# Query and key projections as pairs by seven products, and filler products queued behind attention and scan steps

## The chip, the cores and the metric

The kernel runs on one core of a Trainium2 chip. The metric is the device time of one execution in microseconds. A core has TensorE (PE in the profile), VectorE (DVE), ScalarE (ACT), GpSimd (POOL) and SyncE (SP); here SyncE issues every transfer, all on one queue. SBUF and PSUM are the on-chip memories, PSUM with eight banks that matmuls write.

## The reference

One inference step of one layer over 1024 new and 64 running rows (T = 1088), width 1024:

```
xn = rmsnorm(x);  z, xBC, dt, q, k, v, g_ssm, g_att = split(xn @ w_in)
xBC = silu(causal_conv4(xBC) + bias);  dt = softplus(dt + bias)
y = ssd_scan(x, dt, B, C, chunks of 64) ; y = rmsnorm((y + D*x) * silu(z)) per group
q, k = partial_rope(rmsnorm per head of 64);  16 heads of q and k, 8 of v
o = rmsnorm((softmax(q1 k1) - lam * softmax(q2 k2)) v)       chunk-causal
x += (sigmoid(g_ssm) * (y @ w_bs) + sigmoid(g_att) * (o @ w_ba)) @ w_out
x += (silu(causal_conv3(a)) * b) @ w_down,  a, b = split(rmsnorm(x) @ w_up)
outputs: x, k, v, the last scan states and the last rows of both convolutions
```

Everything is fp32. The kernel writes an fp32 operand as hi + lo (hi rounded to a shorter type) and forms hi·hi, hi·lo and lo·hi, so a product of two blocks is three matmuls.

## The kernel before

Features lie on the 128 partitions and time on the free axis. `xn` (hi and lo) stays in SBUF. A projection of 128 features is a *block*. `project` computes a plain block in three parts (384, 384 and 320 columns), 24 matmuls each.

The stages in order:

1. Norm of x, then `values(0)` and `values(1)`, which also give dt. `steps` turns dt into step sizes, decays and cumulative sums (`dtt`, `nacum`, `decs`).
2. `heads` for q, then for k: eight plain blocks each. The evacuation copies every part from PSUM into a row `qr` (ten buffers of T columns in the pool `qk`), squares it and sums the squares over the blocks. After the eighth block the whole tensor is normed at once: a matmul with `blk`, `rstd_of`, a product per row, the rotation on rows 0 and 1, the split into hi and lo, and the stores to `q_st` or `k_st` in DRAM. Between the two the cached keys are split likewise. k's rows use the same ten buffers.
3. `differences` forms sums and differences of quarters of `xn` for a seven-product scheme (Winograd's form of Strassen's). `values(2)` and `values(3)` run beside it.
4. Twenty *pairs*: two blocks together (`seven`), of z or of x, B and C. Per pair there are seven products `p` on two column halves `s`, 168 matmuls of 272 columns. The weights' seven left factors (`left_blocks`) are made one pair ahead by GpSimd, ScalarE and VectorE. `Gated` applies silu to z and stores it in `z_sc`; `Conv` convolves and stores in `x_sc`.
5. Attention: eight heads, nine steps each in `ATT_ORDER`. A step is scores (matmuls into `sc`), maximum, exponentials, difference, transposes (`pt`), weighted sum (`po`). `fill(rate)` hands out parts of the *filler* beside the steps: the 16 gate blocks, 48 parts.
6. Scan: 36 steps, with a `front` (transposes `tr`, `cb`) and a `back` (`yi`, `ye`, `stp`) each. The filler goes on with the remaining gates, then with the branch products of o and of the first half of y.
7. The last branch, the output projection and the feed-forward part.

The Tile framework orders each engine's instructions by a simulated timeline, in which program order is the priority: work whose inputs are ready can move ahead of work that waits. That decides where filler matmuls stand between the steps of attention and the scan. Engines then work through their queues in that order.

Of the kernel before, what the change touches and what calls it, by code (L numbers as in the profile page):

```python
# [17 lines left out]
P = 128  # L18
# [23 lines left out]
WMAX = 4 * (256 + 16)  # L42
# [15 lines left out]
ATT_STEPS = 0.53  # L58
SCAN_STEPS = 1.08
MID = dict(fa=8, fs=2, fu=4, pr=6, cc=4)  # L60
MIDW = 552


def group(g):
# [4 lines left out]
PAIRS = [p for i in range(4) for p in (("c", CONV[6 * i], CONV[6 * i + 1]), ("z", 4 * i, 4 * i + 1),  # L69
                                       ("c", CONV[6 * i + 2], CONV[6 * i + 3]),  # L70
                                       ("c", CONV[6 * i + 4], CONV[6 * i + 5]), ("z", 4 * i + 2, 4 * i + 3))]
# [8 lines left out]
def hybrid_layer(ctx: ExitStack, tc: tile.TileContext, xT, prm, cst, rope, wvd, win, wbs, wba, wout, wup, wdn,  # L80
# [12 lines left out]
    b_sc = scratch("b_sc", [2 * P, 4 * T // 2])  # L93
    q_st, k_st = (scratch(n, [2 * D, T]) for n in ("q_st", "k_st"))
# [43 lines left out]
    def weights(block, k, m, pool=None):  # L138
        nonlocal turn
        if pool is None:  # L140
            turn = (turn + 1) % 3
        p, b = (pool, 1) if pool is not None else (extra, 1) if extra is not None and turn == 0 else (wp, 2)
        w = p.tile([P, WMAX], F32, name="w_f", tag="w_f", bufs=b)
        hi = p.tile([P, WMAX], R32, name="w_hi", tag="w_hi", bufs=b)
        lo = p.tile([P, WMAX], R32, name="w_lo", tag="w_lo", bufs=b)
# [79 lines left out]
    nacum, decs = (dq.tile([P, 9, 32], F32, name=n) for n in ("nacum", "decs"))  # L225
    dtt = dq.tile([P, 2, 9, 32], F32, name="dtt")
    dt_tok, dtw = dtt[:, 0], dtt[:, 1]
# [10 lines left out]

    st = tc.alloc_tile_pool(name="st", bufs=1, side="right")
    extra = tc.alloc_tile_pool(name="wx1", bufs=1, side="right")  # L240
    first = tc.alloc_tile_pool(name="wx0", bufs=1, side="right")
# [53 lines left out]
    two = [values(0, dtw), values(1, dtw, (extra, first))]  # L295
# [4 lines left out]
    first.release()  # L300

    with tc.tile_pool(name="qk", bufs=1) as qk:
        rp = qk.tile([P, 2, T], F32, name="rp")
        load(out=rp, in_=rope)
        wq8 = qk.tile([P, 8], F32, name="wq8")
        V.tensor_scalar_mul(wq8, par[:, O_QN : O_QN + 8], 0.125)

        def row(name, w=T):
            t = qk.tile([P, T], F32, name=name, tag="qr", bufs=QR)
            return t[:, :w]  # L310

        def split_out(src, j, n, to):
            hi = qk.tile([P, T], R32, name="qh", tag="qh", bufs=2)[:, :n]
            lo = qk.tile([P, T], R32, name="ql", tag="ql", bufs=2)[:, :n]
            S.copy(hi, src)
            V.tensor_tensor(out=lo, in0=src, in1=hi, op=ALU.subtract)
            for u, t in enumerate((hi, lo)):
                load(out=to[D * u + P * j : D * u + P * (j + 1), :], in_=t.bitcast(F32))

        def heads(blk0, wcol, to, plain):  # L320
            ss = row("ss")
            rows = [row("qr") for _ in range(KT)]

            def block(j):
                r = rows[j]

                def evac(ps, c, w):
                    S.copy(r[:, c : c + w], ps)
                    if j == 0:
                        act(ss[:, c : c + w], ps, AF.Square)  # L330
                    else:
                        sq = qk.tile([P, 384], F32, name="qsq", tag="qsq", bufs=QSQ)
                        act(sq[:, :w], ps, AF.Square)
                        V.tensor_tensor(out=ss[:, c : c + w], in0=ss[:, c : c + w], in1=sq[:, :w], op=ALU.add)

                return project(win[blk0 + j], evac)

            tiles = [block(j) for j in range(KT)]
            run(chain(*tiles))
            rs = qk.tile([P, T], F32, name="qrs", tag="qrs")  # L340
            for c, w in WIDE:
                ps = stat(w)
                PE.matmul(ps, blk, ss[:, c : c + w], start=True, stop=True)
                rstd_of(qk, rs[:, c : c + w], ps, w, "qn", 1.0 / 64)
            def finish(j):
                if plain is not None:
                    load(out=plain[P * j : P * (j + 1), :], in_=rows[j])
                split_out(rows[j], j, T, to)

            for j in range(2, KT):  # L350
                V.scalar_tensor_tensor(rows[j], rows[j], wcol(j), rs, ALU.mult, ALU.mult)
                finish(j)
            for j in range(2):
                V.scalar_tensor_tensor(rows[j], rows[j], wcol(j), rs, ALU.mult, ALU.mult)
            for c in (0, T // 2):
                cs = slice(c, c + T // 2)
                t1 = qk.tile([P, T // 2], F32, name="t1", tag="t1")
                t2 = qk.tile([P, T // 2], F32, name="t2", tag="t2")
                x1, x2, co, si = rows[0][:, cs], rows[1][:, cs], rp[:, 0, cs], rp[:, 1, cs]
                V.tensor_tensor(out=t1, in0=x2, in1=si, op=ALU.mult)  # L360
                V.tensor_tensor(out=t2, in0=x1, in1=si, op=ALU.mult)
                V.tensor_tensor(out=x1, in0=x1, in1=co, op=ALU.mult)
                V.tensor_tensor(out=x1, in0=x1, in1=t1, op=ALU.subtract)
                V.tensor_tensor(out=x2, in0=x2, in1=co, op=ALU.mult)
                V.tensor_tensor(out=x2, in0=x2, in1=t2, op=ALU.add)
            for j in range(2):
                finish(j)

        def steps():
# [29 lines left out]
            af = row("af")[:32]  # L399
# [9 lines left out]
        heads(B_Q, lambda j: wq8[:, j : j + 1], q_st, None)  # L409
        for j in range(KT):  # L410
            ck = row("ck", PAST)
            load(out=ck, in_=ckT[P * j : P * (j + 1), :])
            split_out(ck, j, PAST, c_st)
        heads(B_K, lambda j: col(O_KN + j), k_st, kT)
    extra.release()
    extra = None
    st.release()
# [14 lines left out]
    def left_blocks(b0, b1, row):  # L432

        a = []
        for b in (b0, b1):
            w = wp.tile([P, WMAX], F32, name="w_f", tag="w_f", bufs=2)
            load(out=w[:, :1024], in_=b)
            a += [w[:, :512], w[:, 512:1024]]
        q11, q12, q21, q22 = a
        s1, s2 = (row("fs", n)[:, :512] for n in ("ws1", "ws2"))  # L440
# [3 lines left out]
        def own(src):  # L444
            hi, lo = (row("fa", n, R32)[:, :512] for n in ("wh", "wl"))
            split(hi, lo, src)
            return hi, lo
# [16 lines left out]
    tu = tc.alloc_tile_pool(name="tu", bufs=1)  # L464
    mid = tc.alloc_tile_pool(name="mid", bufs=1)

    def mrow(tag, name, dt=F32):
        return mid.tile([P, MIDW], dt, name=name, tag=tag, bufs=MID[tag])

    X = {}  # L470
    for s in range(2):
        X["b11", s], X["b21", s], X["b22", s], X["t1", s] = quarter(0, s), quarter(1, s), quarter(1, 2 + s), quarter(0, 2 + s)
        for n in ("t2", "t3", "t4"):
            X[n, s] = [tu.tile([P, 4, QW], R32, name=f"{n}{s}{u}") for u in range(2)]
    for u in range(2):
        for k in range(4):
            load(out=b_sc[P * u : P * (u + 1), T // 2 * k : T // 2 * (k + 1)], in_=xn[u][:, k, T // 2 :].bitcast(F32))

    def differences(s, j, late):

        js = slice(2 * j, 2 * j + 2)

        def whole(tag, kh, q, eng):
            t = couple(mrow(tag, "xf"))
            hi, lo = (x[:, js].bitcast(F32) for x in quarter(kh, q))
            eng.tensor_tensor(out=t, in0=hi, in1=lo, op=ALU.add)
            return t

        def part(n, src):
            hi, lo = X[n, s]  # L490
            split(hi[:, js], lo[:, js], src)

        f12, f11 = whole("pr", 0, 2 + s, V), whole("fa", 0, s, G)
        V.tensor_tensor(out=f11, in0=f12, in1=f11, op=ALU.subtract)
        f22 = whole("pr", 1, 2 + s, V)
        t2 = couple(mrow("cc", "t2"))
        V.tensor_tensor(out=t2, in0=f22, in1=f11, op=ALU.subtract)
        part("t2", t2)
        G.tensor_tensor(out=f12, in0=f22, in1=f12, op=ALU.subtract)
        part("t3", f12)  # L500
        f21 = whole("cc", 1, s, G)
# [896 lines left out]
```

## Time and profile before

| | us |
|---|---|
| median of 3 runs (lowest, highest) | 2709.69 (2709.1, 2713.98) |
| profiled execution | 2707.97 |
| its span | 2706.2 |
| TensorE busy | 2461.8 |
| VectorE busy | 1652.7 |
| ScalarE busy | 1157.4 |
| GpSimd busy | 681.3 |
| mean granted TensorE clock | 0.958 |

The page's first part gives the busy time of an engine; a busy TensorE is not one at its peak, since matmuls overlap. Its second part cuts the span into 40 slices and shows busy shares in tenths. A window row reads: stretch, its length, then per engine the busy time and the number of instructions, the granted TensorE clock, the share of the DMA engines and the GB/s moved. A wait row reads: engine, tile and line that waited, whom for, us in total, times, longest. A group row reads: line, engine, operation, output<-inputs, shape, count, then busy us and mean ns of one, then idle time ahead.

### The profile page before, as it was taken

The page shows a single profiled execution, that of the slowest core. Times are in us where ns is not written, and L with a number is a line of the kernel's source. Part 1 is how long each engine was busy: PE and PEld are TensorE (multiplying, and loading weights), DVE is VectorE, ACT ScalarE, POOL GpSimd, SP SyncE. Part 2 cuts the span into 40 slices and gives each one's busy share as a digit, 9 for nine tenths or more (in the row PEclk, how much of TensorE's full clock was granted, in tenths as well). Part 3 has the DMA queues.
Part 4 walks back from the last instruction along what each step waited for, and adds up shares of the span by engine and source line. Part 5 has one row for each costly group of instructions (what it writes and reads, how often), then busy time and mean ns, then how long its engine had stood idle before and what let it go on. Part 6 is the DMA issues. An engine that isn't in the chain of part 4 may idle for free.

```text
span 2706.2 us, 44595 instructions
## 1 busy us (share of the span) xinstructions
PE 2461.8 (91%) x17126; PEld 2360.7 (87%) x17126; DVE 1652.7 (61%) x2764; ACT 1157.4 (43%) x2453; POOL 681.3 (25%) x652
## 2 busy tenths in 40 slices
PE   8996759999999999877688899699789999999999
PEld 8996759999999999765577788599689999999999
DVE  6334567886784554666377777664686666674322
ACT  5233324444443444455366767422543333442200
POOL 3000043443340000000054443202445555540000
PEclk9998879999999999887899999899889999999999
DMA  6216332233337545443676766565212222246553
GB/s 190 76 64 232 144 119 101 101 101 109 101 105 230 152 131 156 140 131 102 205 245 203 236 193 187 180 194 184 87 60 84 72 84 73 76 141 238 167 152 119
DMA packets 244885, 383.27 MB, mean 142 GB/s; under 512 B 31392, under 2 KB 175648, under 8 KB 244544
## 3 DMA queue, kind: packets, MB, share of 16 engines
q1 hardware_dynamic: 244672, 380.42, 43.6%
q8 instruction: 134, 2.20, 0.3%
q14 instruction: 79, 0.65, 0.1%
HBM read 256.80 MB, written 123.53 MB: 141 GB/s over the span
## 4 chain that ended last, share of the span: by engine, by line
PE 71%; DVE 10%; DMA 7%; ACT 6%; issue 3%; SPq 2%; POOL 1%; DVEq 0%; ACTq 0%; POOLq 0%
PE mx L1182 11%; PE mx L603 11%; PE mm L156 6%; PE mm L157 6%; PE mm L158 6%; PE mx L158 5%; PE mx L156 5%; PE mx L157 5%; PE mm L603 5%; PE mm L1182 5%; PE po L769 2%; DMA kl_t<-k_st 2%; PE sc L722 1%; PE sc L721 1%; ACT bc L875 1%
## 5 line engine op out<-in xcount | busy, mean ns | idle before, releaser
L149 ACT CAST w_hi<-w_f 128x1024 fp32r<-128x1024 f32 (+2 forms) x104 | 107.3, 1033 | 273.0 <-PE mx L157 175.4
L873 POOL TENSOR_SCALAR_AFFINE_SELECT bc<-bc 128x1024 f32<-128x1024 f32 (+1 forms) x36 | 41.3, 1148 | 650.9 <-ACT e L860 647.3
L156 PE MATMUL mm<-xn_hi,w_hi 128*128 128x384 f32 (+1 forms) x528 | 175.0, 332 | 23.5 <-ACT ss L330 23.5
L150 DVE TENSOR_TENSOR w_lo<-w_f,w_hi 128x1024 fp32r<-128x1024 f32 (+2 forms) x104 | 134.9, 1298 | 71.7 <-ACT w_hi L149 71.2
L156 PE MATMUL mm<-b_hi,w_hi 128*128 128x384 f32 (+1 forms) x448 | 154.6, 346 | 23.5 <-DVE b_g L200 16.2
L158 PE MATMUL mm<-xn_hi,w_lo 128*128 128x384 f32 (+1 forms) x528 | 175.9, 333 | 0.0
L157 PE MATMUL mm<-xn_lo,w_hi 128*128 128x384 f32 (+1 forms) x528 | 175.1, 332 | 0.0
L157 PE MATMUL mm<-b_lo,w_hi 128*128 128x384 f32 (+1 forms) x448 | 151.1, 337 | 18.7 <-DMA b_lo<-o_sc 18.4
L158 PE MATMUL mm<-b_hi,w_lo 128*128 128x384 f32 (+1 forms) x448 | 150.4, 336 | 0.0
L1182 PE MATMUL mx<-n,wh 128*128 128x272 f32 x752 | 145.4, 291 | 3.2 <-ACT wh L1031 1.5
L1182 PE MATMUL mx<-m,w_hi 128*128 128x272 f32 x760 | 144.2, 288 | 0.0
L735 ACT ACTIVATE p_t<-sc,mx 128x1024 f32<-128x1024 f32 (+5 forms) x144 | 106.3, 740 | 72.5 <-PE pt L750 21.5
L585 DVE SCALAR_TENSOR_TENSOR cc<-pre,par,cc 128x544 f32<-128x544 f32 (+1 forms) x144 | 131.7, 941 | 0.4
L1182 PEld LDWEIGHTS mx<-n,wh 128*128 128x128 f32 x752 | 119.7, 191 | 3.9 <-ACT wh L1031 1.7
L156 PEld LDWEIGHTS mm<-xn_hi,w_hi 128*128 128x128 f32 x528 | 100.0, 189 | 24.6 <-ACT ss L330 23.8
L1182 PEld LDWEIGHTS mx<-m,w_hi 128*128 128x128 f32 x760 | 119.4, 188 | 0.0
L1199 POOL TENSOR_TENSOR hb<-hb,cc 128x544 f32<-128x544 f32 (+2 forms) x66 | 89.3, 1366 | 116.5 <-ACT w_hi L1031 97.7
L156 PEld LDWEIGHTS mm<-b_hi,w_hi 128*128 128x128 f32 x448 | 86.5, 193 | 30.5 <-issue 20.8
L158 PE MATMUL mx<-m,w_lo 128*128 128x272 f32 (+2 forms) x356 | 109.0, 308 | 1.5 <-DVE w_lo L150 1.5
L1182 PE MATMUL mx<-m,w_lo 128*128 128x272 f32 x380 | 109.5, 288 | 0.0
L1182 PE MATMUL mx<-n,wl 128*128 128x272 f32 x376 | 108.9, 291 | 0.4 <-DVE wl L1032 0.4
L157 PE MATMUL mx<-m,w_hi 128*128 128x272 f32 (+2 forms) x356 | 109.1, 307 | 0.0
(399 smaller groups left out, 8513.0 us busy)
## 6 DMA issues: line engine op xcount, KB each, us to landing
w_f<-in_win_dram SPq DMA_DIRECT2D x76, 512.0 KB, 3.5
w_f<-in_wup_dram SPq DMA_DIRECT2D x44, 512.0 KB, 3.5
bc<-a_sc SPq DMA_DIRECT2D x32, 512.0 KB, 6.4
h_sc<-hb SPq DMA_DIRECT2D x44, 272.0 KB, 2.1
hr<-h_sc SPq DMA_DIRECT2D x44, 272.0 KB, 5.2
xa<-x_sc SPq DMA_DIRECT2D x48, 192.0 KB, 2.5
z_sc<-pre SPq DMA_DIRECT2D x32, 272.0 KB, 2.2
kh_t<-k_st SPq DMA_DIRECT2D x32, 272.0 KB, 7.3
```

What stands on the lines that cost most here:

```text
L149: S.copy(hi, w)
L150: V.tensor_tensor(out=lo, in0=w, in1=hi, op=ALU.subtract)
L156: PE.matmul(ps, a_hi, b_hi, start=i == 0, stop=False)
L157: PE.matmul(ps, a_hi, b_lo, start=False, stop=False)
L158: PE.matmul(ps, a_lo, b_hi, start=False, stop=i == n - 1)
L585: V.scalar_tensor_tensor(cc, t[:, i : i + n], cw(i), cc, ALU.mult, ALU.add)
L603: PE.matmul(ps, w[x][:, c], b[y][:, k], start=start and k == i == 0, stop=k == 3 and i == 2, skip_group_check=not start)
L735: act(p_t[:n, :nk], sc[c][:n, :nk], AF.Exp, bias=mx[:n, c : c + 1], accum_out=dst)
L769: PE.matmul(po[:n, :P], a_t[b // 4][:kw, b % 4 * P : b % 4 * P + n], rhs, start=b == 0, stop=b == nb - 1)
L873: G.affine_select(bc[:L, :, :L], bc[:L, :, :L], [[0, 8], [1, L]], ALU.is_ge, -1e30, base=0, channel_multiplier=-1)
L1182: PE.matmul(ps, w[x][:, c], b[y][:, k], start=start and k == i == 0, stop=k == 3 and i == 2, skip_group_check=not start)
L1199: G.tensor_tensor(out=hb[h][:, o : o + n], in0=hb[h][:, o : o + n], in1=cc[:, d : d + n], op=ALU.mult)
```

## The change

q and k are no longer plain blocks. After all four `values` come 28 pairs in the order `SEVENS`, in which q, k, z and convolution pairs alternate. A new class `Headed` takes q and k pairs: each finished half row is squared, the squares are summed (on GpSimd, not VectorE), and the row goes raw to DRAM (`r_sc`); rows 0 and 1 are rotated first. After the last q pair, and the last k pair, `finish` makes the scales and then reads the 16 half rows back one by one, norms, splits and stores them; `next(finishing)` after every product lets at most seven half rows, or rows of the cached keys, into a pair. The half of `xn` that t1 replaces is saved to `b_sc` as before, and t1 comes in by way of DRAM (`t_sc`). The step sizes go to DRAM (`d_sc`) and are read back ahead of the scan. `fill` now takes an instruction behind which the part's matmuls must stand on TensorE: in attention the last score matmul of the newest step, in the scan the newest `cb` matmul. The rates go from 0.53 to 0.48 and from 1.08 to 1.12 parts a step. The first values have three weight pools of their own.

```diff
-ATT_STEPS = 0.53
-SCAN_STEPS = 1.08
-MID = dict(fa=8, fs=2, fu=4, pr=6, cc=4)
+ATT_STEPS = 0.48
+SCAN_STEPS = 1.12
+LEFT = dict(fa=8, fs=2)
+MID = dict(fu=4, pr=6, cc=4, ss=2, fr=2)
...
+SEVENS = "qcqzqcq" + "zczc" + "kckckck" + "zczczc" + "cczz"
...
+    for u in range(2):
+        load(out=b_sc[P * u : P * (u + 1), :].rearrange("p (a t) -> p a t", a=4), in_=xn[u][:, :4, HALF:].bitcast(F32))
+    for f in (2, 3):
+        run(values(f))
...
+    def fourth(src):
+        for u in range(2):
+            load(out=xn[u][:, :4, HALF:].bitcast(F32), in_=src[P * u : P * (u + 1), :].rearrange("p (a t) -> p a t", a=4))
+
+    fourth(t_sc)
...
+    class Heads:
...
+        def keep(self, j, h, t):
+            load(out=r_sc[self.kind][P * j : P * (j + 1), HALF * h : HALF * (h + 1)], in_=t)
+
+        def squares(self, h, t):
+            if h not in self.ss:
+                self.ss[h] = mrow("ss", "ss")[:, :HALF]
+                act(self.ss[h], t, AF.Square)
+            else:
+                sq = mrow("cc", "sq")[:, :HALF]
+                act(sq, t, AF.Square)
+                G.tensor_tensor(out=self.ss[h], in0=self.ss[h], in1=sq, op=ALU.add)
...
+        def finish(self):
+            for h in range(2):
+                for s in range(2):
+                    at = self.ss[h][:, QW * s : QW * (s + 1)]
+                    ps = acc(QW)
+                    PE.matmul(ps, blk, at, start=True, stop=True)
+                    rstd_of(mid, at, ps, QW, "qn", 1.0 / 64, t=[mrow("cc", "qn") for _ in range(2)])
+            for h in range(2):
+                for j in range(KT):
+                    x = mrow("fr", "raw")[:, :HALF]
+                    load(out=x, in_=r_sc[self.kind][P * j : P * (j + 1), HALF * h : HALF * (h + 1)])
+                    if j < 2:
+                        V.tensor_tensor(out=x, in0=x, in1=self.ss[h], op=ALU.mult)
+                    else:
+                        V.scalar_tensor_tensor(x, x, self.wcol(j), self.ss[h], ALU.mult, ALU.mult)
+                    if self.plain is not None:
+                        load(out=self.plain[P * j : P * (j + 1), HALF * h : HALF * (h + 1)], in_=x)
+                    hi, lo = (mrow("cc", n, R32)[:, :HALF] for n in ("qh", "ql"))
+                    split(hi, lo, x)
+                    for u, t in enumerate((hi, lo)):
+                        load(out=self.to[D * u + P * j : D * u + P * (j + 1), HALF * h : HALF * (h + 1)], in_=t.bitcast(F32))
+                    yield
...
+    begin = [(p, s) for p in (0, 2, 1, 3, 5, 4, 6) for s in range(2)]
...
+    for n, (kind, f, g) in enumerate(order):
...
+        for p, s in begin if n == 0 else both:
             u.send((p, s))
             if s == 1:
                 nxt += [x for x in [next(coming, None)] if x is not None]
+                next(finishing, None)
...
+        if kind in heads and f == 6:
+            finishing = heads[kind].finish() if kind == "q" else chain(heads[kind].finish(), cached())
...
-    def fill(rate):
+    def fill(rate, behind=None):
         nonlocal spare
         spare += rate
         while spare >= 1:
-            next(filler, None)
+            with tc.issue_after(behind) if behind is not None else nullcontext():
+                next(filler, None)
             spare -= 1
...
-                next(unit)
+                behind = next(unit)
...
-                fill(ATT_STEPS)
+                fill(ATT_STEPS, behind)
...
-            fill(SCAN_STEPS)
+            fill(SCAN_STEPS, marks[-1])
```

Two places show how instructions move. The first is TensorE in attention, behind the transposes of the sixth head's output: `sc` are a step's scores, `po` its weighted sum, `pt` its transposes. Before:

```order
L750 MATMUL pt<-con,p_t 128x128 x8
L769 MATMUL po<-v_t,a_t 128x128 x4
L721 MATMUL sc<-kh_t,q_t 128x512
L722 MATMUL sc<-kl_t,q_t 128x512
L721 MATMUL sc<-kh_t,q_t 128x256
L722 MATMUL sc<-kl_t,q_t 128x256
L769 MATMUL po<-v_t,a_t 128x128 x4
L750 MATMUL pt<-con,p_t 128x128
```

The same place now, where `mm<-xn,w` are products of a gate part:

```order
L810 MATMUL pt<-con,p_t 128x128 x8
L829 MATMUL po<-v_t,a_t 128x128 x4
L781 MATMUL sc<-kh_t,q_t 128x512
L782 MATMUL sc<-kl_t,q_t 128x512
L781 MATMUL sc<-kh_t,q_t 128x256
L782 MATMUL sc<-kl_t,q_t 128x256
L170 MATMUL mm<-xn_hi,w_hi 128x384
L171 MATMUL mm<-xn_lo,w_hi 128x384
L172 MATMUL mm<-xn_hi,w_lo 128x384
```

Where the weighted sum followed the scores at once, a part of the filler now begins behind them. Before, the gate parts stood almost all among the first heads, and none among the later ones up to the last; now 28 parts stand among the last seven heads, three to five in each up to the last, which has two. 40 parts stand ahead of the scan's first `cb`, and eight behind it.

The second is VectorE where q is normed. Before, at the end of q's blocks, `qr` are q's rows (1088 columns), `qrs` the scales, `ql` the lo parts and `w_lo` those of k's weights:

```order
L221 SCALAR_TENSOR_TENSOR qn_1941<-st,qn_1941 128x320
L222 SCALAR_TENSOR_TENSOR qrs<-qn_1941,qn_1942 128x320
L351 SCALAR_TENSOR_TENSOR qr<-qr,wq_1120,qrs 128x1088 x6
L354 SCALAR_TENSOR_TENSOR qr<-qr,wq_1120,qrs 128x1088 x2
L316 TENSOR_TENSOR ql<-qr,qh 128x1088
L150 TENSOR_TENSOR w_lo<-w_f,w_hi 128x1024
```

Now, in the z pair behind the last q pair, `raw` are half rows read back, `ss` the scales, `wl` left factors of the next pair and `u` and `pre` sums of the pair's products (shown with buffer numbers):

```order
L371 TENSOR_TENSOR wl_3849<-w_f_3722,wh_3848 128x512
L371 TENSOR_TENSOR ql_3774<-raw_3770,qh_3773 128x544
L661 TENSOR_TENSOR u1_3692<-mx_3779,u1_3692 128x272
L371 TENSOR_TENSOR ql_3815<-raw_3811,qh_3814 128x544
L661 TENSOR_TENSOR u1_3692<-mx_3793,u1_3692 128x272
L371 TENSOR_TENSOR wl_3889<-w_f_3724,wh_3888 128x512
L588 TENSOR_TENSOR pre_3914<-mx_3901,u1_3692 128x272
L588 TENSOR_TENSOR pre_3914<-mx_3916,u1_3692 128x272
L588 TENSOR_TENSOR pre_3958<-mx_3945,u1_3692 128x272
L533 SCALAR_TENSOR_TENSOR raw_3852<-raw_3852,wq8_1849,ss_1956 128x544
L588 TENSOR_TENSOR pre_3958<-mx_3960,u1_3692 128x272
L533 SCALAR_TENSOR_TENSOR raw_3892<-raw_3892,wq8_1849,ss_1956 128x544
```

The block of whole rows became single half rows, spread over about four pairs between the sums of products.

More of the change, by code (lines that the diff above doesn't have):

```diff
@@ L294, in hybrid_layer @@
     V.memset(dtw[TS:, 8], 0.0)
-    two = [values(0, dtw), values(1, dtw, (extra, first))]
+    two = [values(0, dtw, (extra, first[0])), values(1, dtw, first[1:])]
     for _ in range(9):
@@ L299, in hybrid_layer @@
     quick = None
-    first.release()
+    for p in first[::-1]:
+        p.release()
+    tu = tc.alloc_tile_pool(name="tu", bufs=1)
+    tt = tc.alloc_tile_pool(name="tt", bufs=1)
     with tc.tile_pool(name="qk", bufs=1) as qk:
[L303 to L367, printed above, removed]
@@ L408, in hybrid_layer @@
         steps()
[L409 to L417, printed above, removed]
+        load(out=d_sc, in_=dts.rearrange("p a b c -> p (a b c)"))
+    dp.release()
     def half(h):
```

227 lines of the change are left out of this document (145 added, 82 removed).

## The prediction

> **What bounds the kernel now.** I read the page's parts 1 and 2 first.
>
> ```profile
> PE 2461.8 (91%) x17126; PEld 2360.7 (87%) x17126; DVE 1652.7 (61%) x2764; ACT 1157.4 (43%) x2453; POOL 681.3 (25%) x652
> ...
> PEclk9998879999999999887899999899889999999999
> ```
>
> TensorE is the busiest, and its granted clock dips where its busy share dips. Then the windows, cut where TensorE starts and stops:
>
> ```profile
> core 0: us, PE busy (x) PEld busy (x) DVE busy (x) ACT busy (x) POOL busy (x), PEclk, DMA share, GB/s
> ...
> 204.50:228.00 23.50, 0.00 (x0) 0.00 (x0) 16.95 (x20) 8.27 (x12) 0.00 (x0) 0.58 1.01 389
> 228.00:320.90 92.90, 92.88 (x582) 92.00 (x582) 33.26 (x47) 34.59 (x68) 0.00 (x0) 0.98 0.28 103
> 320.90:351.00 30.10, 0.01 (x1) 0.00 (x0) 21.04 (x24) 7.00 (x8) 0.26 (x1) 0.55 0.95 380
> 351.00:408.40 57.40, 41.95 (x313) 41.41 (x314) 39.33 (x41) 19.37 (x39) 31.12 (x20) 0.82 0.21 66
> 408.40:831.00 422.60, 422.60 (x3362) 421.37 (x3361) 322.82 (x506) 189.63 (x338) 164.64 (x192) 1.00 0.31 105
> 831.00:1328.00 497.00, 437.14 (x2685) 397.66 (x2683) 279.59 (x680) 242.12 (x676) 0.00 (x0) 0.93 0.51 146
> 1328.00:1344.20 16.20, 0.01 (x1) 0.02 (x1) 0.23 (x1) 0.21 (x1) 0.00 (x0) 0.60 1.06 357
> 1344.20:1737.60 393.40, 350.85 (x2353) 303.84 (x2353) 286.97 (x360) 253.25 (x564) 167.09 (x104) 0.96 0.66 212
> 1737.60:1753.90 16.30, 0.10 (x2) 0.08 (x1) 7.91 (x18) 4.96 (x13) 0.00 (x0) 0.59 0.42 135
> ```
>
> The 20 pairs by seven products (408.4 to 831.0) are solid TensorE work: 21.13 us a pair. Ahead of them it stands still twice, and the waits of that stretch name whose results were late:
>
> ```profile
> PE mx L156 <- ACT vo L287: 34.2, 2, 30.1
> PE mm L156 <- ACT ss L330: 23.5, 1, 23.5
> ```
>
> Both are copies out of PSUM whose buffers are held by q and k rows still being normed, split and stored (DMA share 1.01 and 0.95). Attention (831 to 1328) and the scan (1344 to 1737.6) lose time in small pieces.
>
> **The change, part by part.** *Stops ahead of the pairs.* q and k become 8 more pairs, and the norming of q runs beside z and convolution pairs, that of k likewise, so no projection waits for it. The idle time is 23.5 + 30.1 + (57.40 - 41.95 = 15.4) = 69.0 us. Half clock: 0.82 over 57.4 us is 20.7 us at half speed, of which 5.2 busy; 0.98 over 92.9 us is 3.7. Half of these 8.9 us, 4.5, was lost.
>
> *Products.* Starts of full-rate products of 384 columns, then of a pair's 272 (first and last row, 20 and 10 products later):
>
> ```profile
> 149.69 0.33 PE L158 MATMUL mm<-xn_hi,w_lo 128*128 128x384 f32 x1
> ...
> 153.16 0.33 PE L157 MATMUL mx<-xn_lo,w_hi 128*128 128x384 f32 x1
> ```
>
> ```profile
> 499.76 0.28 PE L603 MATMUL mx<-xn_lo,wh 128*128 128x272 f32 x1
> ...
> 501.01 0.29 PE L603 MATMUL mm<-xn_hi,wl 128*128 128x272 f32 x1
> ```
>
> So 0.1735 and 0.125 us; between them, 0.146 for 320 columns. A plain block is 24 x (0.1735 + 0.1735 + 0.146) = 11.83 us, 3.94 a part. Two blocks take 23.65, a pair 21.13; eight pairs save 8 x 2.52 = 20.2 us. Together 69.0 + 4.5 + 20.2 = 93.7 us off.
>
> *What comes back there.* The differences, the step sizes and the first weights now lie beside the last values. Before, the same differences left 15.4 us idle; now 51 us of value products (432 of 256 columns, about 0.119 each by the same line) cover VectorE's 39.3. I take 8 us, between 0 and 20. The trip of t1 through DRAM is covered: five of the first pair's seven products, 15 us, stand ahead of the one that reads it.
>
> VectorE gets the norming. Three pairs of before, convolution, z, convolution:
>
> ```profile
> 429.40:450.60 21.20, 21.20 (x170) 21.09 (x169) 18.09 (x27) 9.26 (x17) 9.90 (x10) 1.00 0.36 122
> 450.60:471.70 21.10, 21.10 (x171) 21.10 (x170) 12.40 (x23) 9.16 (x16) 6.51 (x11) 1.00 0.24 86
> 471.70:492.90 21.20, 21.20 (x170) 21.09 (x170) 20.76 (x33) 10.77 (x19) 10.22 (x11) 1.00 0.30 103
> ```
>
> VectorE at 20.76 of 21.20 still delays nothing. The nearest operations to the new ones, from the groups of that stretch:
>
> ```profile
> L585 DVE SCALAR_TENSOR_TENSOR cc<-pre,par,cc 128x547 f32<-128x547 f32 x72 | 77.8, 1093 | 0.0
> ...
> L585 DVE SCALAR_TENSOR_TENSOR cc<-pre,par,cc 128x544 f32<-128x544 f32 x72 | 56.8, 788 | 0.4
> ...
> L452 POOL TENSOR_TENSOR w_f<-w_f 128x512 f32<-128x512 f32 x19 | 30.0, 1579 | 0.0
> ...
> L427 DVE TENSOR_TENSOR w_lo<-ws,w_hi 128x512 fp32r<-128x512 f32 x40 | 27.7, 693 | 3.2 <-ACT w_hi L426 0.4
> ...
> L547 ACT ACTIVATE pre<-pre 128x544 f32<-128x544 f32 x23 | 15.1, 657 | 23.4 <-DVE pre L543 23.4
> ```
>
> A half row costs VectorE 0.788 + 0.693 = 1.48 us; at most seven are let into a pair, 10.4 us. A z pair then holds 12.4 + 10.4 = 22.8, a convolution pair 18.1 + 10.4 = 28.5: over by 1.7 and 7.4, for q and for k, 18.2 in all. Neighbouring z pairs with few rows take some back, the rotation (24 operations, 19 us in two places) adds some. I take 15 us, between 0 (all spread out) and 45 (the rows' four scratch buffers hold up the copies too). ScalarE, at 9 to 11 of 21 us, hides its share, and the transfers a DMA share of 0.3. This part: -93.7 + 8 + 15 = -70.7 us.
>
> *Attention.* Two heads, one full of gate products and two without:
>
> ```profile
> 905.00:980.00 75.00, 73.43 (x477) 70.19 (x477) 37.14 (x84) 34.37 (x92) 0.00 (x0) 1.00 0.48 143
> ...
> 1169.00:1216.00 47.00, 33.24 (x188) 26.95 (x188) 30.98 (x83) 25.35 (x76) 0.00 (x0) 0.85 0.50 135
> 1216.00:1263.50 47.50, 34.48 (x189) 28.49 (x188) 31.20 (x83) 25.38 (x77) 0.00 (x0) 0.78 0.49 134
> ```
>
> The first holds 477 - 189 = 288 products, 12 parts of 24, 47.3 us: its own work is 27 us, and TensorE is the bound. The later ones are bound by the steps' chain, at 47 us, with TensorE waiting and at reduced clock. So the gates were spent early. How many there were:
>
> ```profile
> L156 PEld LDWEIGHTS mm<-xn_hi,w_hi 128*128 128x128 f32 x376 | 70.7, 188 | 0.3
> ```
>
> 376 / 8 = 47 parts of 48. In the changed order 40 stand ahead of the scan: 12 up to the first head's output, then 28 over seven heads, 4 each (15.8 us), behind a step's scores. A head's floor is 27 + 15.8 = 42.8 on TensorE and 47 by its chain. Its ceiling is 56: the cost of filling starts near nothing and ends at one for one, so it stays under the straight line from 47 (none) to 74 (47.3 us of it). I take 51.5, the middle. First head and parts ahead: 74 before, one part less now, 70; an end of 7. 70 + 7 x 51.5 + 7 = 437 against 497: -60 us (-91 at 47, -28 at 56).
>
> TensorE's granted clock is 0.85 and 0.78 in the unfilled heads. [...] The trace doesn't show that the 47 us chain shrinks with the clock, so I don't go below 47.
>
> *Scan.* It takes over 7 parts, 27.6 us. The 16.2 us stop at 1328 goes, since gates stand there now, but its loads (DMA share 1.06) remain: 10 us at the start, where the gates must queue behind the first step, and 8 where the branch's rows are loaded later. Of the 42.6 us idle in 1344 to 1737.6, I let 10 be filled; the stop at 1737.6 stays. 27.6 - 16.2 + 18 - 10 = +19 us, between 0 (the parts all fall into idle time) and +45 (both stops return, nothing is filled). Reloading the step sizes is part of the 10.
>
> *Sum.* The profiled execution took 2707.97 us for a span of 2706.2; the median of the runs is 1.7 above it. 2708.0 - 70.7 - 60 + 19 + 1.7 = 2598 us. What follows the scan is unchanged.
>
> **The rivals.** *Everything hides*: heads at 47, no new stalls, scan unchanged: 2709.7 - 93.7 - 91 = 2525. For it: VectorE at 98% of a pair delayed nothing. Against: 28.5 us of work in 21.1.
>
> *Fill gets in the way*: a part of 3.94 us ahead of a step's transposes lengthens the chain: heads at 56, scan +45: 2709.7 - 70.7 - 28 + 45 = 2656. For it: the chain was already 47 of which TensorE's share waits in line.
>
> *VectorE loses to GpSimd.* The 28 new sums of squares run on GpSimd; the form of L585 that meets GpSimd's work takes 1093 ns on average against 788. If each sum holds VectorE for its whole 1.58 us, and none of it is slack: +44, 2642. Against: q and k pairs have no convolution. [...]
>
> *Slower: the row chain holds the queues.* A half row goes load, product, cast, difference, store:
>
> ```profile
> hr<-h_sc SPq DMA_DIRECT2D x44, 272.0 KB, 5.2
> ...
> z_sc<-pre SPq DMA_DIRECT2D x32, 272.0 KB, 2.2
> ```
>
> 5.2 + 0.79 + 0.66 + 0.69 + 2.2 = 9.5 us. All transfers go out on one queue, weights behind rows, and VectorE's instructions stand in order; if rows ran one at a time and pairs waited for them, each of 40 (32, and 8 of the cache) would cost 9.5 instead of the 3.0 that a seventh of a pair hides: +260 for my 15, 2843 us. It turns the sign from (111.7 + 15) / 40 = 3.2 us over the 3.0, 6.2 us a row. Against it: two buffers for rows, and rows of the order that stand two by two between products' sums.
>
> **How the numbers follow.** Forecast 0.53, everything hides 0.12, fill in the way 0.17, GpSimd 0.09, row chain 0.06, the bad ends of all terms together (+20 - 8, +45 - 15, heads at 56, scan +45: 2698) 0.03. The forecast's own ends are half the terms' ranges, 2560 to 2635. The range from 2535 to 2665 takes in the fill and GpSimd cases and leaves out the row chain, the worst mixture and most of the first rival. Faster by over 0.2% (5 us, about what this kernel's runs can tell from no change) 0.91, within it 0.02, slower 0.07.
>
> **What would show it.** Right: TensorE starts pairs near 408.4 - 69.0 - 4.5 - 16 x 11.83 + 8 = 154 us and ends them near 154 + 28 x 21.13 + 15 = 761, without a stop over 10 us before; pairs of 21.1 us apart from those behind the last q and k pair; heads of nearly equal length, about 51, at a clock above 0.95; the scan some 20 us longer. Wrong: pairs that wait for VectorE all along, a head near 60, or stops at the scan's start over 20 us.

## The result: 0.7 per cent faster, a sixth of what was forecast

The changed kernel takes 2692.95 us (median of 5 runs, 2687.68 to 2698.51) against 2709.69 before: ratio 0.9934, 95% interval 0.9915 to 0.9954. Faster, as predicted, but by 17 us and not by 112: the time lies 28 us above the upper end of the range. The profiled execution took 2688.88 us for a span of 2687.1.

The page of the changed kernel, parts 1 and 2:

```profile
PE 2469.8 (92%) x17322; PEld 2365.5 (88%) x17322; DVE 1701.5 (63%) x2878; ACT 1197.1 (45%) x2510; POOL 775.4 (29%) x712
...
PEclk9999999999999889889789999899889999999999
```

TensorE is busy for 8 us more than before, though eight pairs were priced 20 us below the sixteen plain blocks that they replace. Its stops ahead of the pairs are gone, and so are the clock's 0.8, 0.8 and 0.7 of slices 4 to 6; in attention and at the scan's start (slices 14 to 21) it is at 0.7 to 0.9. Then the windows of the changed kernel, cut at the pairs' start, at the two pairs in which norming begins, at the end of the pairs, of attention and of the scan's first step:

```profile
core 0: us, PE busy (x) PEld busy (x) DVE busy (x) ACT busy (x) POOL busy (x), PEclk, DMA share, GB/s
150.50:300.30 149.80, 148.22 (x1178) 147.56 (x1177) 99.14 (x158) 64.53 (x117) 67.90 (x61) 1.00 0.38 128
300.30:331.60 31.30, 25.30 (x179) 24.32 (x178) 12.84 (x26) 24.28 (x36) 7.68 (x9) 0.95 0.31 111
331.60:557.60 226.00, 216.06 (x1682) 214.02 (x1681) 182.84 (x284) 103.27 (x188) 103.85 (x100) 0.98 0.46 155
557.60:589.40 31.80, 25.28 (x179) 24.02 (x178) 13.40 (x25) 25.67 (x37) 7.94 (x9) 0.95 0.33 116
589.40:796.40 207.00, 195.96 (x1515) 193.35 (x1514) 166.22 (x258) 93.09 (x170) 71.50 (x79) 0.98 0.61 205
796.40:1276.50 480.10, 412.40 (x2456) 372.27 (x2454) 272.62 (x661) 233.15 (x656) 0.00 (x0) 0.90 0.50 139
1276.50:1303.00 26.50, 4.54 (x17) 2.79 (x16) 4.82 (x17) 6.55 (x14) 0.36 (x1) 0.56 0.89 274
1303.00:1723.20 420.20, 386.10 (x2565) 340.74 (x2565) 297.34 (x369) 260.48 (x576) 162.88 (x104) 0.96 0.67 210
1723.20:1731.80 8.60, 0.04 (x1) 0.02 (x1) 5.65 (x13) 3.61 (x8) 0.00 (x0) 0.73 0.88 268
```

Against the windows of before: the pairs end at 796.4 instead of 831 (-35; -71 forecast), attention takes 480.1 instead of 497.0 (-17; -60 forecast), the scan 455.3 instead of 425.9 (+29; +19 forecast), what follows 955.3 instead of 952.3 (+3). Together -19, as the spans have it (2706.2 to 2687.1).

Two single pairs stand out: 31.3 and 31.8 us. Each follows the last q or k pair. In them VectorE, whose overload was forecast, is at 13 us, and **ScalarE** is at 24 to 26. Its timeline in the first of them (start, duration, line, operation):

```profile
304.33 1.28 ACT L232 ACT_TABLE_LOAD   x1
305.62 0.49 ACT L232 ACTIVATE qn<-mx,eps_t 128x272 f32<-128x272 f32 x1
306.19 1.28 ACT L233 ACT_TABLE_LOAD   x1
307.48 0.43 ACT L233 ACTIVATE qn<-qn 128x272 f32<-128x272 f32 x1
307.93 1.28 ACT L232 ACT_TABLE_LOAD   x1
...
320.17 1.28 ACT L586 ACT_TABLE_LOAD   x1
321.46 0.40 ACT L586 ACTIVATE pre<-mx 128x272 f32<-128x272 f32 x1
```

`finish` calls `rstd_of` four times, and each Ln (L232) and each Exp (L233) brings a load of ScalarE's table, the SiLU of the z pair another: nine of 1.28 us. The z pair's copies out of PSUM stand in order behind them, VectorE waits for the scales, and TensorE behind both. Waits in that pair (engine, tile and line, whom for, total, times, longest):

```profile
DVE qn L235 <- ACT qn L234: 9.6, 4, 3.7
...
PE mx L647 <- ACT pre L586: 2.8, 1, 2.8
```

The price stood in the trace of before, in groups that the prediction did not use (these and the changed kernel's, over the whole span):

```profile
L218 ACT ACT_TABLE_LOAD x16 | 20.5, 1283 | 0.3
L219 ACT ACT_TABLE_LOAD x13 | 16.7, 1283 | 0.2
```

```profile
L232 ACT ACT_TABLE_LOAD x24 | 30.8, 1283 | 0.4
L233 ACT ACT_TABLE_LOAD x24 | 30.8, 1283 | 0.5
```

### The profile page after: what moved, and what is told of

It is laid out like the page before. It is cut to its first block, busy times and chain, and to the rows that moved or that the text cites. A ratio compares the mean times of both kernels' runs of the same rounds, so it can differ in the third digit from the quotient of the medians.

```text
span 2687.1 us, 45559 instructions
## 1 busy us (share of the span) xinstructions
PE 2469.8 (92%) x17322; PEld 2365.5 (88%) x17322; DVE 1701.5 (63%) x2878; ACT 1197.1 (45%) x2510; POOL 775.4 (29%) x712
## 4 chain that ended last, share of the span: by engine, by line
PE 42%; DVE 5%; DMA 4%; ACT 4%; issue 1%; SPq 1%; POOL 1%; DVEq 0%; ACTq 0%; POOLq 0%
PE mx L1245 12%; PE mm L1245 5%; PE mm L170 4%; PE mm L172 4%; PE mm L171 4%; PE mx L172 3%; PE mx L170 3%; PE mx L171 3%; PE po L829 1%; ACT bc L938 1%; DVE x L1135 1%; PE yi L947 1%; DVE y L989 1%; DMA b_f<-y_sc 1%; PE ye L953 1%
## 5 line engine op out<-in xcount | busy, mean ns | idle before, releaser
L647 PE MATMUL mx<-t,wh 128*128 128x272 f32 x896 | 179.6, 297 | 18.2 <-DVE u L657 18.2
L163 ACT CAST w_hi<-w_f 128x1024 fp32r<-128x1024 f32 (+2 forms) x88 | 90.6, 1029 | 233.2 <-PE mx L171 135.0
L647 PEld LDWEIGHTS mx<-t,wh 128*128 128x128 f32 x896 | 145.8, 195 | 21.7 <-DVE u L657 20.9
L164 DVE TENSOR_TENSOR w_lo<-w_f,w_hi 128x1024 fp32r<-128x1024 f32 (+2 forms) x88 | 110.3, 1254 | 36.4 <-ACT w_hi L163 35.9
L647 PE MATMUL mx<-t,wl 128*128 128x272 f32 x448 | 132.8, 296 | 0.0
L170 PE MATMUL mm<-xn_hi,w_hi 128*128 128x384 f32 (+1 forms) x360 | 125.2, 348 | 1.3 <-ACT gt L716 1.3
L172 PE MATMUL mm<-xn_hi,w_lo 128*128 128x384 f32 (+1 forms) x360 | 123.1, 342 | 0.0
L171 PE MATMUL mm<-xn_lo,w_hi 128*128 128x384 f32 (+1 forms) x360 | 122.4, 340 | 0.0
L371 DVE TENSOR_TENSOR wl<-w_f,wh 128x512 fp32r<-128x512 f32 x84 | 92.4, 1101 | 40.5 <-ACT wh L370 40.2
```

The source lines that it names most:

```text
L170: PE.matmul(ps, a_hi, b_hi, start=i == 0, stop=False)
L171: PE.matmul(ps, a_hi, b_lo, start=False, stop=False)
L172: PE.matmul(ps, a_lo, b_hi, start=False, stop=i == n - 1)
L647: PE.matmul(ps, w[x][:, c], b[y][:, k], start=start and k == i == 0, stop=k == 3 and i == 2, skip_group_check=not start)
```

## The experiments

**Each half of the change alone.** First the changed kernel with the old fill, then the kernel before with the new fill:

```
-ATT_STEPS = 0.48
-SCAN_STEPS = 1.12
+ATT_STEPS = 0.53
+SCAN_STEPS = 1.08
...
-                fill(ATT_STEPS, behind)
+                fill(ATT_STEPS)
...
-            fill(SCAN_STEPS, marks[-1])
+            fill(SCAN_STEPS)
```

> The changed kernel with the fill of the kernel before: gate products are given to the scheduler with no step to stand behind, at the old rates 0.53 and 1.08. So the projection half of the change alone. Theory of the prediction (the fill half is worth -41 us: attention -60, scan +19): without it the kernel is about 41 us slower than after, near 2734 us. New theory (read from the profile after: pairs end 35 us earlier than before, attention gives 17 and the scan takes 29): the fill half costs about 12 us, so this kernel takes about 2680 us, 12 below after.

> The kernel before with the fill half alone: gate products behind a step's scores or its product of C and B, rates 0.48 and 1.12. Theory of the prediction: -41, near 2669 us. New theory: -17 in attention and +29 in the scan, near 2722 us; heads of 56 to 58 us and a stop of over 20 us at the scan's start as in after.

The first took 2692.28 us (ratio to before 0.9932, interval 0.9918 to 0.9947), the changed kernel's own time; the second 2719.34 (1.0028, 1.0016 to 1.0041), slower than before by 8. So the whole gain is the projections', and the fill half is worth nothing there and costs a little by itself. The forecast of -41 is refuted in both. The new reading (+12) was too dark in one and close in the other. From the end of the pairs to the last transpose of a head's output, the new fill gains 10 us on the kernel before and 17 on the new projections; what follows takes 16 and 20 us more.

**The tables.** Square in place of Ln and Exp, with 71 loads in the changed kernel and 52 in this one:

```
-        act(u, mean, AF.Ln, bias=eps_t[: out.shape[0]], scale=scale)
-        act(r, u, AF.Exp, scale=-0.5)
+        act(u, mean, lut[0], bias=eps_t[: out.shape[0]], scale=scale)
+        act(r, u, lut[1], scale=-0.5)
...
+                            lut=(AF.Square, AF.Square))
```

> The changed kernel with Square in place of Ln and Exp where q and k are normed: the same shapes, counts and operands, but no other table for ScalarE; the scales of the rows of q and k are left out (not the true norms). New theory (9 table loads of 1.28 us in each of the two finishes stretch pairs 8 and 19 from about 21.5 to 31.5): these pairs fall to 22 us and the kernel to about 2673, 20 below after. Rival (the prediction's: VectorE's norming alone stretches the pairs, ScalarE has slack for its share): within 4 us of after, both pairs still above 29 us.

2671.4 us, 21.6 below the changed kernel (0.9851, 0.9834 to 0.9867). The two pairs, in its windows:

```profile
299.00:321.90 22.90, 22.90 (x178) 22.59 (x178) 15.46 (x29) 13.74 (x30) 7.64 (x10) 1.00 0.45 156
546.00:568.90 22.90, 22.90 (x178) 22.58 (x178) 16.00 (x29) 13.52 (x29) 8.43 (x10) 1.00 0.53 184
```

From 31.3 and 31.8 to 22.9, TensorE without a gap, at the same small steps. The next kernel keeps the true norms and changes the order: both Ln ahead of both Exp, each over a whole half row:

```
-                    rstd_of(mid, at, ps, QW, "qn", 1.0 / 64, t=[mrow("cc", "qn") for _ in range(2)])
+                    S.copy(at, ps)
+            t = [[mrow("cc", n)[:, :HALF] for n in ("qu", "qr")] for h in range(2)]
+            for h in range(2):
+                ln = act(t[h][0], self.ss[h], AF.Ln, bias=eps_t, scale=1.0 / 64)
+            with tc.issue_after(ln.ins):
+                for h in range(2):
+                    act(t[h][1], t[h][0], AF.Exp, scale=-0.5)
...
```

> The changed kernel with the same norms in another order of ScalarE's work: the four sums are copied out of PSUM first, then the two Ln of a finish stand together ahead of its two Exp, each over a whole half row. Three table loads in q's finish and five in k's in place of nine and nine. If each load costs what it holds ScalarE (1.28 us, and the kernel with Square gained 21.6 over after by leaving out all): about two thirds of that, 14 us off after's time, near 2679, pairs 8 and 19 near 24 to 26 us. Rival (it was the eight small chained steps Ln, Exp, Square that held the pair and not the tables): the kernel with Square kept those, and lost the stall; so a gain under 5 us here would say that something else than the loads differed there.

2670.14 us (0.9857, 0.9829 to 0.9884): 22.8 off where 14 were expected, all that leaving them out gave, though eight loads remain and the steps are fewer and longer. In its windows q's pair is without a gap again, k's (five loads) not quite:

```profile
298.90:321.80 22.90, 22.90 (x179) 22.59 (x178) 13.10 (x22) 17.14 (x29) 8.24 (x9) 1.00 0.40 136
547.00:573.50 26.50, 24.69 (x178) 24.15 (x177) 14.80 (x25) 19.79 (x31) 8.30 (x9) 0.94 0.36 123
```

**What is left in the norming pairs.** First the rows spread over more pairs, on the changed kernel:

```
-                next(finishing, None)
+                p % 2 or next(finishing, None)
```

> The changed kernel with the normed rows of q and k let in at four of a pair's seven products in place of all seven: the same work over 4 pairs (q) and 6 pairs (k with the cache) in place of 2.3 and 3.4. If bursts make the stalls (VectorE at 23 to 25 of 26 us in the long pairs, and rows loaded into two buffers): the pairs of 25 to 27 us in those zones fall to 22 to 24, 10 to 18 us off, about 2680. Rival (VectorE's sum over the zone is what counts, or the loads stay late whenever they come): within 4 us of after, the same excess over more pairs. Pairs 8 and 19, where the tables change, keep their 31 us.

2693.71 us (0.994, 0.9918 to 0.9962): nothing. Six pairs behind q's finish, 126.8 us at 21.13, take as long, here in the changed kernel and then in this one:

```profile
sum 141.40, PE 131.46 PEld 129.69 DVE 121.70 ACT 65.46 POOL 61.27; mean PE 21.91 PEld 21.62 DVE 20.28 ACT 10.91 POOL 10.21
```

```profile
sum 144.30, PE 131.57 PEld 129.69 DVE 122.90 ACT 65.90 POOL 60.88; mean PE 21.93 PEld 21.62 DVE 20.48 ACT 10.98 POOL 10.15
```

In the same six pairs of the changed kernel VectorE stands, in order, behind rows that have not come from DRAM (total, times, longest):

```profile
DVE raw L533 <- DMA raw<-r_q: 8.1, 3, 3.7
...
DVE raw L531 <- DMA raw<-r_q: 2.8, 2, 2.6
```

So, on the kernel with the tables in order, rows that aren't read back (which takes away their transfers too):

```
-                    load(out=x, in_=r_sc[self.kind][P * j : P * (j + 1), HALF * h : HALF * (h + 1)])
...
-                        V.scalar_tensor_tensor(x, x, self.wcol(j), self.ss[h], ALU.mult, ALU.mult)
+                        V.scalar_tensor_tensor(x, self.ss[h], self.wcol(j), self.ss[h], ALU.mult, ALU.mult)
```

> The kernel with the tables in order, and the rows of q and k not read back from DRAM when they are normed: VectorE's two operations and ScalarE's cast per half row stay, with the scale row as their input, so q and k are not the reference's. If VectorE, in order, stands behind rows that have not come (waits of 8.1 and 2.8 us for the raw rows in six pairs of q's zone after, as many in k's): 15 us below the kernel with the tables in order, and pairs 9 to 14 within 22.5 us. Rival (VectorE's own work of 20 to 23 us a pair is the bound): within 4 us of it, the 27 us pairs stay.

2661.33 us (0.9819, 0.9804 to 0.9835): 8.8 us less, between the two expectations. The zones behind q's and k's finish (six and eight pairs, 295.8 us at 21.13), first in the kernel with the tables in order, then without the loads:

```profile
sum 322.40, PE 302.66 PEld 298.84 DVE 273.62 ACT 152.24 POOL 133.31; mean PE 151.33 PEld 149.42 DVE 136.81 ACT 76.12 POOL 66.66
```

```profile
sum 310.40, PE 298.68 PEld 295.60 DVE 276.54 ACT 153.05 POOL 133.50; mean PE 149.34 PEld 147.80 DVE 138.27 ACT 76.52 POOL 66.75
```

12 of 26.6 us go with the loads, at about the same VectorE work. A third row buffer would test the cure; no run has one. In the 14.6 us that are left TensorE stands idle for 11.7, nearly all behind VectorE's sums of products, here in q's zone and then in k's:

```profile
PE mx L656 <- DVE u L666: 4.5, 3, 1.8
PE mx L656 <- DVE pre L620: 1.5, 2, 1.0
```

```profile
PE mm L656 <- DVE pre L597: 3.3, 2, 1.7
PE mx L656 <- DVE u L666: 1.6, 1, 1.6
```

Whether this is VectorE's load in convolution pairs with rows, the next order tests, again on the kernel with the tables in order and with rows let in at four of a pair's seven products:

```
-SEVENS = "qcqzqcq" + "zczc" + "kckckck" + "zczczc" + "cczz"
+SEVENS = "qcqcqcq" + "zzzz" + "kckckck" + "zzzz" + "cccccc"
...
-                next(finishing, None)
+                p % 2 or next(finishing, None)
```

> The kernel with the tables in order, and besides that the pairs in the order qcqcqcq zzzz kckckck zzzz cccccc, with normed rows at four of a pair's seven products: the rows of q and k meet z pairs only (VectorE 12.4 us of 21 without rows, 18.3 with four) and the convolutions stand last, where nothing is normed. If the stall left in the two zones (about 9 us that go when the rows aren't read back, and another 15) is VectorE's load in convolution pairs with rows: 15 us below the kernel with tables in order, near 2656. Rival (rows come late from DRAM whatever pairs they stand in, since two buffers hold them; or the six convolution pairs in a row overload VectorE themselves): within 5 us of it.

2668.42 us (0.9849, 0.9834 to 0.9864): 1.7 below, not 15. The pairs take 619.8 us instead of 627.1 there, but start 3 later. The rival is nearer: the order of pairs matters little while rows come late. What of VectorE's work makes the sums late stays open.

**What a gate part costs a head: 2.3 us.** Smaller pieces at the same place; another place, between a step's transposes and its products with the values; and both:

```
...
+                if k in (2, 5):
+                    yield
...
-                fill(ATT_STEPS, behind)
+                fill(3 * ATT_STEPS, behind)
```

```
+            yield at_pe
             po = pa.tile([P, 512], F32, name="po", tag="pt", bufs=2)
...
                 behind = next(unit)
                 if last is not None:
+                    behind = next(last)
+                fill(ATT_STEPS, behind)
+                if last is not None:
                     run(last)
...
-                fill(ATT_STEPS, behind)
```

> The changed kernel with each gate part given out in three thirds of 8 products (1.3 us) at three times the rate, so that no more than a third or two stands behind a step's scores; the amounts per head stay (4.2 to 4.4 parts). If a whole part of 3.94 us in one piece lengthens the chain of a step (the prediction's rival of fill in the way): heads fall from 57 to about 51, 7 x 6 = 40 us off, near 2653. Rival (a part costs a head 2.3 to 2.5 us however it stands: 74.5 us with 12 parts before, 57 with 4 after, 47 without): heads stay at 56 to 58 and the time within 5 us of after.

> The changed kernel with a head's gate parts between the transposes of a step and the products with the values that wait for the transposes' copies, in place of behind the scores. If a part costs a head 2.4 us because it stands where TensorE has work ready (scores done, transposes next) and the copies' wait stays empty: a copy's wait of 1 to 2 us is filled by each, heads of 4 parts at 52 to 54, 20 to 35 us off after's time, near 2665. Rival (the loop through softmax and copies is one chain, and any whole part of 3.94 us lengthens it alike): heads 56 to 58, within 6 us of after, 2690.

> The same place, between a step's transposes and its products with the values, and thirds of a part (8 products, 1.3 us) at three times the rate: one or two stand in each wait for copies. If the place and the size count together: heads at 49 to 52, 35 to 50 us below after, near 2650. Rival (cost goes with the amount, 2.4 us a part, wherever it stands; thirds behind scores already changed nothing): heads 55 to 58, within 8 us of after.

2699.75 us (0.9957, 0.9942 to 0.9973), 2706.71 (0.9991, 0.9977 to 1.0004) and 2704.96 (0.9978, 0.9965 to 0.999): 7, 14 and 12 above the changed kernel, where the readings that they tested had them 40, 20 to 35 and 35 to 50 below it. Neither size nor place helps; between transposes and values six heads take 348 us, with whole parts and with thirds, instead of 342. Then the part taken apart: without 21 of its 24 products, and without its side work (weights split once, nothing copied out):

```
+                product(ps, [(w_hi[:, 0], w_lo[:, 0], *(t[:, 0, c : c + w] for t in xn))])
```

```
+        w_hi, w_lo = weights(win[B_G], KT, P)
         for j in tiles:
...
-                act(gt, ps, AF.Tanh, scale=0.5)
-                load(out=g_sc[P * j : P * (j + 1), c : c + w], in_=gt)
+                load(out=g_sc[P * j : P * (j + 1), c : c + w], in_=xn[0][:, j % KT, c : c + w].bitcast(F32))
```

> The changed kernel with 3 of a gate part's 24 products, so the gates aren't the reference's; the weights' load and split, the tanh out of PSUM and the store of every part stay, at the same places and rates. A head's own length without fill is 47 us, with four whole parts 57. If TensorE's products make the 10 us: heads at 47 to 49. Rival (the side work of a part, about 1 us each on VectorE and ScalarE, both of them in the softmax's chain, makes it): heads at 53 to 57.

> The changed kernel with all products of the gates, but one weight block split once for all, nothing copied out of PSUM, and stores of other data of the same size, so the gates aren't the reference's: TensorE's share of the fill without VectorE's and ScalarE's. If the products make the 10 us: heads at 55 to 57. Rival (the side work): heads at 47 to 50.

One run each: 2602.43 and 2665.03 us. Six heads, from the first head's output to the seventh's, in the windows of six kernels in turn: before, changed, thirds, thirds between transposes and values, without products, without side work.

```profile
943.30:1285.70 342.40, 292.00 (x1780) 262.17 (x1780) 200.69 (x497) 172.16 (x490) 0.00 (x0) 0.91 0.47 134
```

```profile
900.30:1242.40 342.10, 293.36 (x1752) 263.76 (x1752) 203.63 (x500) 172.59 (x490) 0.00 (x0) 0.90 0.48 133
```

```profile
902.50:1244.40 341.90, 296.18 (x1752) 265.39 (x1752) 206.51 (x499) 172.76 (x490) 0.00 (x0) 0.88 0.48 132
```

```profile
900.90:1248.70 347.80, 292.37 (x1753) 263.12 (x1752) 204.62 (x500) 170.72 (x491) 0.00 (x0) 0.88 0.48 131
```

```profile
882.10:1180.10 298.00, 220.29 (x1206) 181.47 (x1206) 195.38 (x499) 169.82 (x490) 0.00 (x0) 0.81 0.55 152
```

```profile
887.10:1228.10 341.00, 295.81 (x1752) 266.00 (x1752) 195.30 (x492) 153.61 (x457) 0.00 (x0) 0.91 0.41 106
```

Before put 27 parts into these six heads as 12, 12, 3 and three times none; the change puts 26 as 4, 4, 5, 4, 4, 5. The sum is the same to 0.3 us. A part costs (342.1 - 6 x 47) / 26 = 2.3 us on average, however the parts are spread, and 2.5 where six heads take 348. That holds for sums: the changed kernel's heads with five parts are no longer than those with four (56.9 and 57.1 us on average). The side work is not it (341.0); TensorE's products are (298.0, 49.7 a head). Why a part costs 0.58 of its 3.94 us while TensorE stands idle for 49 us of these heads is not settled: without the products it idles 78 us, so of 73 us more busy time only 29 fall into gaps, in whatever pieces they come.

**The scan's first steps.** The fill behind the step at hand, four parts more at the first:

```
-            fill(SCAN_STEPS, marks[-1])
+            fill(SCAN_STEPS + (0 if n else 4), marks[-2])
```

> The changed kernel with the scan's fill behind the product of C and B of the step at hand, not of the step to come, and four parts more at the first step. If the stop of 24 us between the first two steps' products lasts because the gates must queue behind the second one: it falls under 10 us and the kernel gains 10 to 16 us, about 2680. Rival (the same loads and stores hold the scan's first steps, and whatever fills the stop is lacking later as cover): the stop fills, but the scan ends within 4 us of where it did, 2690.

2687.3 us (0.9917, 0.99 to 0.9935): 5.6 less, between both. From the first to the second step's product of C and B, in the changed kernel and in this one:

```profile
1279.10:1303.00 23.90, 4.50 (x16) 2.75 (x16) 4.47 (x15) 4.07 (x9) 0.36 (x1) 0.52 0.92 287
```

```profile
1280.50:1307.00 26.50, 23.59 (x136) 22.80 (x136) 6.92 (x17) 8.05 (x16) 0.36 (x1) 0.94 0.98 310
```

The stop is filled, but not shorter, and the transfers are busy in both (DMA share 0.92 and 0.98). In the changed kernel they make it: TensorE's second product of C and B waits 17.8 us for a copy by ScalarE, which, in order, stands twice behind attention's last stores (11.6 and 5.4 us), as VectorE does:

```profile
1303.02 0.48 PE L928 MATMUL cb<-con,in 128*128 128x128 f32 x1 [17.80 <-ACT b_cb L931]
```


```profile
DVE ol L855 <- DMA o_sc<-ol: 11.9, 1, 11.9
ACT oh L854 <- DMA o_sc<-oh: 11.6, 1, 11.6
ACT e L923 <- DMA o_sc<-ol: 5.4, 1, 5.4
```

Five parts, 19.7 us of products, put there bring 5.6, and the two intervals overlap. That the others had lain in the later steps' gaps is the likely reason; no run shows it.

**Together**: the tables in order, the convolutions last with rows at four products, this fill.

> Tables in order (22.8 us below after by itself), the pairs in the order with the convolutions last (another 2), and the scan's fill behind the step at hand with four parts more at the first (5.6 by itself). If these add up: 2663 us, 1.7 per cent below before. Rival (the gain at the scan's first steps was the difference of two single builds and not of the place): 2668.

2663.95 us (five runs, 2660.38 to 2666.62; 0.9831, 0.9817 to 0.9844), 29 below the changed kernel, and 4.5 below the run with the first two alone: the parts add up, as far as steps of 2 and 6 us can be told.

## Why the prediction was wrong, by its own steps

**Start of the pairs: right.** 154 us was forecast, 150.5 measured; the stops of 23.5 and 30.1 us are gone, and the longest left ahead of the pairs is 5.3. The half speed behind its 4.5 us is in the trace of before, where the granted clock was 0.50 from 209 to 232 and from 369 to 385. The new projections with the old fill have the whole gain.

**Norming beside the pairs: the first step that failed**, a term of 15 us (0 to 45) that measured 54: from 150.5 to 796.4 are 645.9 us, 28 x 21.13 is 591.6. The sentence that failed is "ScalarE, at 9 to 11 of 21 us, hides its share": it counted squares and casts and not the table loads, nine or ten of 1.28 us in a single pair. They made about 22. Late rows made 9 of the kernel's time and 12 of the two zones', against "and the transfers a DMA share of 0.3"; it is 0.46 and 0.61 in the long stretches. Of the 20 that are left, 14.6 lie in the zones, where TensorE stands behind VectorE's sums; the scales' own products make about 1.8 in each of the two norming pairs, and the first seven pairs, which hold q's rotation, are 1.9 over. So the 15 for VectorE came out near what it was meant for. The rival of the row chain named the mechanism of late rows, at twenty times its size. The rival of GpSimd has no run of its own, and the convolution's products don't show VectorE held for a sum's whole 1.58 us: the 23 slow ones of before took 1.81 us on average, 1.03 more than the others. The traces speak against its 44 us: the two forms of the convolution's product took 1093 and 788 ns before and take 1066 and 833 now, and a half row costs VectorE 0.89 + 0.79 = 1.68 us instead of 1.48, 6 us for all 32.

**Attention: the second.** That "the cost of filling starts near nothing and ends at one for one" is wrong, and it was the largest miss. The cost is near a line from the first parts on: 47 us with none, 52.6 with 3 (before's third), 57 with 4 or 5, 74.5 with 12, 1.9 to 2.3 a part. Then spreading cannot gain, and the -17 are about the seven parts that left attention, 7 x 2.3 = 16. Why it is a line stays open. Heads come out at 55 to 60, where the rival of fill in the way had 56, but its mechanism, one long piece in a step's chain, isn't it: thirds change nothing. The forecast had the heads at a clock above 0.95; the six heads of the windows above show a mean of 0.90, against 0.91 before, and TensorE idle for 49 of 342 us. So an even fill left the gaps, and a clock no higher than before.

**Scan: within its range, not by its own terms.** +29 against +19, within 0 to 45. The stop at the start came back (26.5 us where 10 were allowed), the one at the end shrank (8.6 instead of 16.3, where none of it was forecast).

**The sum.** Missed by 36 us in the pairs, 43 in attention, 10 in the scan, 3 behind it, and 2 because the median lies 4.1 above the profiled execution and not 1.7: 2693 for 2598, within a microsecond of rounding. That a gain remained rests on the one part that held, the start of the pairs. The mixture of all bad ends stood at 2698 with a chance of 0.03: the terms were treated as if they failed separately, and two of them shared one flaw, a price taken from engines' busy time and not from what stands in line.

## To carry to other kernels

Where a step is moved between work that uses other functions, list ScalarE's functions in their new order and price each change of table by the trace's own load; three in q's norming pair hid, nine in a row in front of a PSUM copy didn't, and all Ln ahead of all Exp is a small edit. Before work is spread more evenly, draw its cost against its amount from the stages that the trace already has: a straight line means that spreading gains nothing. And a stop that is filled can give much less than its filler takes, here 5.6 us for 19.7: ask what the filler cost where it stood before.

## What the runs showed of the hardware

Where q and k are normed, the program loads a table before every Ln and every Exp in turn (over the span, before 24 of the 30 Ln and 24 of the 30 Exp of `rstd_of`); q's norms with both Ln ahead of both Exp took two loads instead of eight. A load takes 1283 ns in these rows. In 67 of the changed kernel's 71 the next operation starts 0.01 us after the load's end, all but the first of the 71 start within 0.1 us of the end of the operation before, and leaving out 19 of them saved 21.6 us, 1.1 each.

Some of VectorE's convolution products took longer beside GpSimd's sums. Of the 144 before (L585), 23 take 1.7 to 1.8 us, and each of these shares time with a GpSimd sum of 512 columns; the other 121 take 0.77 to 0.79, though 22 of them share 0.62 to 0.69 us with such a sum. In the changed kernel, sums of 272 columns with one input in PSUM (L657) take 0.43 us with GpSimd beside them (24) and without (32).

Kernels with the same code for the pairs end them between 796.4 and 801.7 us. The order isn't the reason: in the changed kernel, the one with the old fill and three of the other fill kernels, TensorE, VectorE and ScalarE have the same instructions in the same order up to there. So here a single stage of a single profiled execution is not to be read closer than 5 us, and the 12 us of the late rows and the 7 of the new order of pairs above are to be taken with that.
